# One row of each norm's weights, spread by products with ones, and read-back rows taken one job sooner

## The chip, the core and the metric

The kernel runs on one core of a Trainium2 chip. The metric is the device time of one execution in microseconds, the median over the runs shown. The engines in the text are TensorE (PE, with its weight loads PEld), VectorE (DVE), ScalarE (ACT), GpSimd (POOL) and SyncE (SP, which here issues most of the transfers).

## The reference, cut to what matters

One decoder block on 512 tokens of 1024 values. Two token mixers are merged; their sum with the input goes through a layer norm (LN1). A mixture of 32 experts follows, two experts per token, and a second layer norm (LN2) ends the block.

```python
def layer_norm(x, g, b):
    xf = x.astype(jnp.float32)
    mu = xf.mean(-1, keepdims=True)
    var = jnp.square(xf - mu).mean(-1, keepdims=True)
    return ((xf - mu) * lax.rsqrt(var + LN_EPS) * g.astype(jnp.float32) + b.astype(jnp.float32)).astype(x.dtype)
...
    x = layer_norm(ALPHA * x + merged @ w_out[layer], ln1_g[layer], ln1_b[layer])
    ffn = hier_moe(x, w_group[layer], b_group[layer], w_router[layer], b_router[layer],
                   w_gate[layer], w_up[layer], w_down[layer])
    x = layer_norm(ALPHA * x + ffn, ln2_g[layer], ln2_b[layer])
```

Each of `ln1_g`, `ln1_b`, `ln2_g`, `ln2_b` is one vector of 1024 values. In the kernel a token lies on a partition, so such a vector is wanted on all 128 partitions alike.

## The kernel before

The expert stage takes up the second half of the time. `work` lists 17 jobs, n = 0 to 16: w = 0 to 7, then "ov" (tokens beyond an expert's capacity), then w = 8 to 15. A job w serves experts w and w + 16, with 64 tokens each. It needs six pieces of 1 MB of weights, four up (`w_up`) and two down (`w_dn`). `stage(w)` issues their loads on SP's queue three jobs ahead, each into the next of a ring of pages of 128x2048. Behind the six pieces of w = 15 it issues the two loads of LN2's weights, the last on SP before the output's.

A job's parts on PE have these names in the trace: the up projection `mm<-wexp,xg`; two turns of the hidden activation, `mm<-ident,h`; the transposes of the next job's tokens, `qt<-ident,xg`; the down projection `pv<-wexp,hT`. What a job yields reaches the tokens' rows in one of two ways. Jobs w = 0 to 9 scatter it to `yp` in DRAM (POOL's queue). Jobs w = 10 to 15 combine: the products `qt<-four,ct` put the rows in their places, sixteen of them in eight parts, and DVE adds each part to `acc` (L1293). These parts run during the next job (`late`). "qt" is a ring of four PSUM banks (`qk_bank`), shared by combine products and transposes, so a product waits until an older bank has been read.

The scattered rows come back block by block (b = 0 to 3, 128 tokens each): `back_load` sets a page to zero and gathers twice into it on POOL's queue (L1270, L1271), and `back_add` adds the two halves on DVE (L1278). `BACK_AT` and `BACK_ADD` name the jobs behind which this is written. LN1's weights are applied to `acc` by DVE in jobs 3 to 6 (L1570, L1571). LN2's are `g2`, used from the last job's end on (`centre`, `finish` and `rest`, recorded under L111, as everything else of the last job). In the last job each combine part is added with a running sum (`sums`), LN2's mean follows from these, and block by block the output is written.

The order of instructions on an engine is fixed when the kernel is built: a scheduler places what is written without a fixed place; each engine then works its list in order. A load on SP waits until its page is free and until an older load of its semaphore (eight in turn) has landed.

## Time and profile before

| | |
|---|---|
| median of 3 runs | 690.48 us (690.04 to 690.83) |
| the profiled execution | 689.77 us |
| its span, first to last instruction | 688.0 us |
| PE busy | 648.0 us, 94% |
| DVE busy | 402.8 us, 59% |
| ACT busy | 271.9 us, 40% |
| moved by all queues | 163.23 MB, mean 237 GB/s |

Busy shares are means over the whole span. How PE and the transfers stand to each other in the expert stage is read from windows of that stage, and the end of the kernel from the timelines.

### The profile page before, as it was taken

The page shows a single profiled execution, that of the slowest core. Times are in us where ns is not written, and L with a number is a line of the kernel's source. Part 1 is how long each engine was busy: PE and PEld are TensorE (multiplying, and loading weights), DVE is VectorE, ACT ScalarE, POOL GpSimd, SP SyncE. Part 2 cuts the span into 40 slices and gives each one's busy share as a digit, 9 for nine tenths or more (in the row PEclk, how much of TensorE's full clock was granted, in tenths as well). Part 3 has the DMA queues.
Part 4 walks back from the last instruction along what each step waited for, and adds up shares of the span by engine and source line. Part 5 has one row for each costly group of instructions (what it writes and reads, how often), then busy time and mean ns, then how long its engine had stood idle before and what let it go on. Part 6 is the DMA issues. An engine that isn't in the chain of part 4 may idle for free.

```text
span 688.0 us, 9318 instructions
## 1 busy us (share of the span) xinstructions
PE 648.0 (94%) x3366; PEld 429.1 (62%) x3366; DVE 402.8 (59%) x1016; ACT 271.9 (40%) x600; POOL 105.8 (15%) x111
## 2 busy tenths in 40 slices
PE   8999998999999999999999999999998998998880
PEld 5797886766688887878799993334433342443330
DVE  5785999877455344387725567567224521573783
ACT  5663431859355445464313333122122121322360
POOL 0100000000030000002311002221222120550092
PEclk9999999999999999999999999999999999999995
DMA  8472511011581110243886688999999999999502
GB/s 319 150 258 73 202 62 61 1 62 61 184 306 62 62 62 17 81 149 127 341 329 238 242 315 342 409 418 417 419 420 417 420 420 417 417 416 415 236 31 111
DMA packets 32028, 163.23 MB, mean 237 GB/s; under 512 B 6675, under 2 KB 7963, under 8 KB 16108
## 3 DMA queue, kind: packets, MB, share of 16 engines
q1 hardware_dynamic: 21324, 139.59, 51.2%
q0 software_dynamic: 8560, 19.88, 7.9%
q10 hardware_dynamic: 2096, 3.15, 1.5%
q8 instruction: 27, 0.44, 0.3%
q14 instruction: 21, 0.17, 0.1%
HBM read 156.62 MB, written 17.33 MB: 253 GB/s over the span
## 4 chain that ended last, share of the span: by engine, by line
PE 56%; DMA 26%; DVE 12%; ACT 2%; issue 1%; POOL 1%; SPq 0%; POOLq 0%; ACTq 0%; DVEq 0%
DMA wexp<-in_w_up_dram 10%; DMA wexp<-in_w_dn_dram 10%; PE mm L189 9%; PE mm L191 8%; PE mm L190 8%; PE mm L1118 5%; PE mm L111 3%; DVE pgS L459 3%; PE pv L1118 3%; DVE mx L457 2%; DMA ln<-in_ln_b_dram 2%; PE pv L589 2%; DVE whl L186 2%; DMA wraw<-in_w_in_dram 2%; PE tr L671 1%
## 5 line engine op out<-in xcount | busy, mean ns | idle before, releaser
L1118 PE MATMUL mm<-wexp,xg 128*64 128x512 f32 x448 | 111.9, 602 | 5.5 <-DMA wexp<-in_w_up_dram 5.5
L189 PE MATMUL mm<-xh,whl 128*128 128x512 f32 (+1 forms) x264 | 104.5, 396 | 0.0
L191 PE MATMUL mm<-xh,whl 128*128 128x512 f32 (+1 forms) x264 | 102.6, 389 | 0.0
L190 PE MATMUL mm<-xl,whl 128*128 128x512 f32 (+1 forms) x264 | 102.4, 388 | 0.0
L1118 PEld LDWEIGHTS mm<-wexp,xg 128*64 128x64 f32 x448 | 33.2, 137 | 64.5 <-issue 53.8
L1118 PE MATMUL pv<-wexp,hT 128*64 128x512 f32 x240 | 57.9, 603 | 0.3
L189 PEld LDWEIGHTS mm<-xh,whl 128*128 128x128 f32 x264 | 49.8, 189 | 10.6 <-issue 2.2
L191 PEld LDWEIGHTS mm<-xh,whl 128*128 128x128 f32 x264 | 49.6, 188 | 10.3 <-issue 0.8
L190 PEld LDWEIGHTS mm<-xl,whl 128*128 128x128 f32 x264 | 49.8, 188 | 9.1 <-issue 1.6
L186 DVE TENSOR_TENSOR whl<-wraw,whl 128x1024 fp32r<-128x1024 f32 x34 | 41.5, 1220 | 22.6 <-ACT whl L185 20.8
L1173 ACT ACTIVATE h<-mm 128x256 f32<-128x256 f32 x14 | 5.4, 384 | 100.0 <-PE mm L1118 100.0
L185 ACT ACTIVATE whl<-wraw 128x1024 fp32r<-128x1024 f32 x34 | 35.7, 1053 | 15.3 <-DMA wraw<-in_w_in_dram 11.7
L1175 DVE TENSOR_TENSOR h<-h,mm 128x256 f32<-128x256 f32 x14 | 5.9, 421 | 58.4 <-ACT h L1173 58.4
L1118 PEld LDWEIGHTS pv<-wexp,hT 128*64 128x64 f32 x240 | 18.3, 139 | 32.3 <-issue 29.0
L831 POOL TENSOR_TENSOR tg<-tg 128x512 f32<-128x512 f32 x8 | 12.1, 1517 | 142.0 <-issue 122.5
L1142 ACT ACTIVATE xg<-qt,ln1c 128x128 f32<-128x128 f32 x76 | 28.2, 462 | 12.6 <-PE qt L1118 12.4
L641 DVE CUSTOM_DVE_ANT_0 La<-qk,bias 128x128 f32<-128x128 f32 (+3 forms) x32 | 15.3, 489 | 30.2 <-PE qk L640 27.6
L748 POOL DMA_DIRECT2D yp<-routes x8 | 5.9, 1109 | 153.7 <-DVE routes L735 153.7
L457 DVE MAX8 mx<-pgS 128x8 f32<-128x256 f32 (+2 forms) x48 | 26.6, 554 | 0.7
L1126 POOL MEMSET xg<- 128x1024 f32 x14 | 13.3, 950 | 87.3 <-PE qt L1118 82.6
L1293 DVE TENSOR_TENSOR acc<-acc,qt 128x512 f32<-128x512 f32 x40 | 24.9, 682 | 2.3 <-PE qt L1118 2.2
L111 PE MATMUL mm<-woh,merged 128*128 128x256 f32 x128 | 26.2, 292 | 0.0
(374 smaller groups left out, 1364.0 us busy)
## 6 DMA issues: line engine op xcount, KB each, us to landing
wexp<-in_w_up_dram SPq DMA_DIRECT2D x64, 1024.0 KB
wexp<-in_w_dn_dram SPq DMA_DIRECT2D x31, 1024.0 KB
wraw<-in_w_in_dram SPq DMA_DIRECT2D x16, 1024.0 KB
yp<-routes POOLq DMA_DIRECT2D x8, 512.0 KB, 6.0
braw<-in_w_br_dram SPq DMA_DIRECT2D x4, 1024.0 KB
woraw<-in_w_out_dram SPq DMA_DIRECT2D x4, 1024.0 KB
xraw<-in_xT_dram SPq DMA_DIRECT2D x4, 512.0 KB
skb<-dra POOLq DMA_DIRECT2D x1, 2048.0 KB
```

The source lines that it names most:

```text
L111: i = f(*a, **k)
L185: nc.scalar.activation(hi, raw, AF.Copy)
L186: nc.vector.tensor_sub(lo, raw, hi.bitcast(F32))
L189: nc.tensor.matmul(o, a[0], b[0], start=start, stop=False)
L190: nc.tensor.matmul(o, a[0], b[1], start=False, stop=False)
L191: nc.tensor.matmul(o, a[1], b[0], start=False, stop=stop)
L457: pin(nc.vector.max(out=mx, in_=acc))
L459: pin(nc.vector.match_replace(out=acc, in_to_replace=mx, in_values=acc, imm_value=GONE))
L641: nc.vector.tensor_tensor_reduce(Ls[b], o, ta_bias[h][:, T - n:], 1.0, -3.0e38, ALU.add, ALU.max, m4[:, b:b + 1])
L1118: return lambda *a, **k: (pin if self.n else (lambda i: i))(getattr(nc.tensor, f)(*a, **k))
L1142: nc.scalar.activation(c, src, AF.Identity, scale=g, bias=b_)
L1293: nc.vector.tensor_add(a, a, pc)
```

## The change

LN1's and LN2's weights are no longer loaded to 128 partitions (two loads of 128x1024, 512 KB each, from a source read 128 times). `row_load` brings each vector to one partition (two loads of 1x1024, 4 KB each, into the same page). `row_spread` makes a row of 128 ones on DVE, multiplies it with 512 values of the row at a time on PE (four products, one partition deep, 128x512 out, in banks of the "qt" ring), and ACT copies each result over the page. LN1's spread is written at the end of job 2, LN2's at the end of job 13. Independently, the read-back of blocks 2 and 3 is written one job sooner, and so are all four adds.

```diff
@@ -71,8 +71,9 @@
 
 SCATTER = tuple(range(10))
 K_EARLY = 1
-BACK_AT = {11: (0, 1), 13: (2, 3)}
-BACK_ADD = {13: (0, 1), 14: (2,), 15: (3,)}
+BACK_AT = {11: (0, 1), 12: (2, 3)}
+BACK_ADD = {12: (0,), 13: (1, 2), 14: (3,)}
+LN2_AT = 13
 X1_AT = 3
 LAST_N = (0, 1, 1, 2, 1, 2, 1, 0)
 P_TR = 0
@@ -1384,11 +1385,25 @@
             pg = functools.partial(gather, idx[:, w:w + 1]) if w else None
             load_pieces(6 * w + 6)
             if w == 15:
-                norm2.append(page(F32, "ln2"))
-                nc.sync.dma_start(norm2[0][:, 0:D], bcast(ln2_g, D))
-                nc.sync.dma_start(norm2[0][:, D:2 * D], bcast(ln2_b, D))
+                norm2.append(row_load(ln2_g, ln2_b))
             es = (w, w + 16)
             jobs[w] = (pg, [ups[e] for e in es], [dns[e] for e in es], tok[:, w:w + 1], wsl[:, w:w + 1])
+
+    def row_load(g, b):
+
+        t = page(F32, "ln")
+        for z, v in enumerate((g, b)):
+            nc.sync.dma_start(t[0:1, z * D:(z + 1) * D], v.rearrange("(o d) -> o d", o=1))
+        return t
+
+    def row_spread(t):
+
+        o = temp(F32, "one")[0:1, 0:P]
+        nc.vector.memset(o, 1.0)
+        for c in range(4):
+            ps = qk_bank()
+            nc.tensor.matmul(ps, o, t[0:1, c * T:(c + 1) * T], start=True, stop=True)
+            nc.scalar.activation(t[:, c * T:(c + 1) * T], ps, AF.Copy)
 
     rows_of = {}
 
@@ -1561,9 +1576,11 @@
                 y = down_proj(hT, dn, w_)
                 late = combine(places(tk_), y, then if n + 2 == len(work) else None)
         if n == X1_AT - 2:
-            g1 = page(F32, "ln1")
-            nc.sync.dma_start(g1[:, 0:D], bcast(ln1_g, D))
-            nc.sync.dma_start(g1[:, D:2 * D], bcast(ln1_b, D))
+            g1 = row_load(ln1_g, ln1_b)
+        if n == X1_AT - 1:
+            row_spread(g1)
+        if n == LN2_AT:
+            row_spread(norm2[0])
         if 0 <= n - X1_AT < NB:
 
             a = acc[n - X1_AT]
```

On PE the list of before at jobs 13 and 14 reads as follows (`mm<-wexp,xg 64x512 x16` is one job's up projection, `pv` its down projection; the second one is job 14's).

```order
2169 L1118 MATMUL mm<-wexp,xg 64x512 x16
2170 L1118 MATMUL qt<-four,ct 128x512 x8
2171 L1118 MATMUL mm<-ident,h 128x128 x2
2172 L1118 MATMUL qt<-four,ct 128x512 x8
2173 L1118 MATMUL qt<-ident,xg 128x128 x8
```

Of the changed kernel it reads, at the same job 14:

```order
2171 L1119 MATMUL mm<-wexp,xg 64x512 x16
2172 L1119 MATMUL mm<-ident,h 128x128 x2
2173 L1405 MATMUL qt<-ln,one 128x512 x4
2174 L1119 MATMUL qt<-four,ct 128x512 x16
2175 L1119 MATMUL qt<-ident,xg 128x128 x8
```

LN2's four products (`qt<-ln,one`) stand behind the turns of h, and all sixteen combine products, eight of which stood ahead of the turns, now stand behind them.

On DVE, from job 13's hidden activation to the last job's first partial sum, before (`acc<-acc,back` are the adds of read-back rows, two for each block, `acc<-acc,qt` the combine's):

```order
753 L1175 TENSOR_TENSOR h<-h,mm 128x256
754 L1293 TENSOR_TENSOR acc<-acc,qt 128x512 x8
755 L1282 TENSOR_SCALAR ct<-iot,tok 128x512
756 L1278 TENSOR_TENSOR acc<-acc,back 128x1024 x2
...
769 L1218 SCALAR_TENSOR_TENSOR four<-pv,wsl,four 128x512 x2
770 L1278 TENSOR_TENSOR acc<-acc,back 128x1024 x2
771 L1293 TENSOR_TENSOR acc<-acc,qt 128x512 x2
772 L1278 TENSOR_TENSOR acc<-acc,back 128x1024 x2
773 L111 TENSOR_TENSOR g_5465<-iot,routes 128x128 x4
774 L111 ISA acc,sums<-acc,qt 128x512
```

And of the changed kernel, from the same place:

```order
754 L1176 TENSOR_TENSOR h<-h,mm 128x256
755 L1294 TENSOR_TENSOR acc<-acc,qt 128x512 x2
756 L1279 TENSOR_TENSOR acc<-acc,back 128x1024
757 L1294 TENSOR_TENSOR acc<-acc,qt 128x512
758 L1279 TENSOR_TENSOR acc<-acc,back 128x1024
759 L1294 TENSOR_TENSOR acc<-acc,qt 128x512 x5
...
767 L1294 TENSOR_TENSOR acc<-acc,qt 128x512 x8
768 L1279 TENSOR_TENSOR acc<-acc,back 128x1024 x2
769 L1219 SCALAR_TENSOR_TENSOR four<-pv,wsl,four 128x512 x2
770 L1176 TENSOR_TENSOR h<-h,mm 128x256
```

The adds of block 0 moved in among job 13's eight combine adds, and the last two pairs moved out of the last job, ahead of job 15's hidden activation. SP's and POOL's lists keep their order.

## Rows read from the trace of the kernel before

**Rows 1.** The page's first line: span and instructions.
```profile
span 688.0 us, 9318 instructions
```

**Rows 2.** Windows: per stretch busy us (count) by engine, granted clock, DMA share, GB/s.
```profile
540.00:580.00 40.00, 36.38 (x170) 14.69 (x171) 10.93 (x30) 9.24 (x22) 7.93 (x8) 0.96 1.02 418
580.00:620.00 40.00, 40.00 (x184) 19.07 (x180) 23.44 (x36) 10.65 (x26) 20.31 (x20) 1.00 1.02 417
620.00:640.00 20.00, 17.79 (x82) 8.30 (x82) 7.62 (x14) 5.44 (x14) 0.00 (x0) 1.00 1.01 414
640.00:642.00 2.00, 2.00 (x11) 0.71 (x12) 0.00 (x0) 2.00 (x7) 0.00 (x0) 1.00 0.86 356
...
650.00:652.00 2.00, 0.79 (x4) 0.00 (x0) 1.98 (x6) 0.00 (x0) 0.00 (x0) 1.00 0.15 61
652.00:654.00 2.00, 1.29 (x4) 0.59 (x6) 1.96 (x7) 1.31 (x3) 0.59 (x1) 0.77 0.03 10
654.00:656.00 2.00, 2.00 (x5) 0.50 (x2) 1.54 (x7) 2.00 (x4) 2.00 (x3) 0.50 0.00 0
656.00:658.00 2.00, 2.00 (x8) 0.73 (x6) 1.26 (x4) 2.00 (x5) 2.00 (x2) 0.87 0.02 4
```

**Rows 3.** The chain that ended last, 560 to 690: start, us, what.
```profile
635.63 15.52 DMA ln<-in_ln_b_dram
```

**Rows 4.** PE's timeline from 590: start, us, instructions, [idle before <- what ended it].
```profile
617.61 2.12 PE L1118 MATMUL qt<-four,ct 128*128 128x512 f32 x8
619.56 1.18 PE L1118 MATMUL qt<-ident,xg 128*128 128x128 f32 x8
...
630.68 3.65 PE L1118 MATMUL mm<-wexp,xg 128*64 128x512 f32 x14 [1.89 <-DMA wexp<-in_w_up_dram]
...
638.75 1.26 PE L1118 MATMUL qt<-ident,xg 128*128 128x128 f32 x8 [0.32 <-DVE acc L1293]
...
643.42 1.89 PE L111 MATMUL mm<-wexp,xg 128*64 128x512 f32 x8
...
652.71 0.92 PE L111 MATMUL qt<-four,ct 128*128 128x512 f32 x2 [1.92 <-DVE sums L111]
```

**Rows 5.** DVE's timeline, from 450 (first row) and from 590.
```profile
455.90 2.35 DVE L1570 TENSOR_TENSOR acc<-acc,ln 128x1024 f32<-128x1024 f32 x2
...
599.86 4.87 DVE L1293 TENSOR_TENSOR acc<-acc,qt 128x512 f32<-128x512 f32 x8
...
608.44 1.23 DVE L1278 TENSOR_TENSOR acc<-acc,back 128x1024 f32<-128x1024 f32 x1 [1.78 <-DMA back<-yp,bidx]
...
645.05 2.47 DVE L1278 TENSOR_TENSOR acc<-acc,back 128x1024 f32<-128x1024 f32 x2
...
648.76 2.48 DVE L1278 TENSOR_TENSOR acc<-acc,back 128x1024 f32<-128x1024 f32 x2
...
661.64 0.47 DVE L111 SCALAR_TENSOR_TENSOR h<-h,wsl,mm 128x256 f32<-128x256 f32 x1
```

**Rows 6.** SP's timeline from 440, and one of its waits (us, times, longest).
```profile
608.67 3.60 SPq L789 DMA_DIRECT2D wexp<-in_w_dn_dram  x2
...
627.69 3.33 SPq L789 DMA_DIRECT2D wexp<-in_w_dn_dram  x2
633.21 0.33 SPq L1388 DMA_DIRECT2D ln<-in_ln_g_dram  x1
635.63 0.33 SPq L1389 DMA_DIRECT2D ln<-in_ln_b_dram  x1
```
```profile
SPq L1388 <- DMA wexp<-in_w_dn_dram: 2.0, 1, 2.0
```

**Rows 7.** Groups by line and form: busy us, mean ns of one, idle before.
```profile
L406 PE MATMUL qk<-ohp,relx 33*8 33x512 f32 x2 | 1.0, 589 | 0.0
...
L1217 ACT ACTIVATE four<-pv,wsl 128x512 fp32r<-128x512 f32 x10 | 7.0, 703 | 11.7 <-PE pv L1118 11.7
```

## The prediction

> **What bounds the kernel now.** I start at the profiled execution's own time, 689.77 us: a span of 688.0 [rows 1] and 1.77 us around it. The sum below is made against the span; the median of the runs shown, 690.48, lies 0.7 above that execution.

> Next come the windows. From 540 to 640 us the DMA share is 1.01 to 1.02 and 414 to 418 GB/s move, while PE is busy 36.38 of 40, 40.00 of 40 and 17.79 of 20 us [rows 2]. So in the middle of the expert stage both are near full, and the transfers are slightly the tighter: the chain that ended last runs through expert weights up to 635.63, and then through the last LN2 load for 15.52 us, to 651.15 [rows 3]. After 640 the stream of weights dries up, unevenly: the share is 0.86 at 640 to 642, 0.15 at 650 to 652, 0.03 at 652 to 654 [rows 2]. Some engines have nothing left more than ten microseconds before others.

> PE's timeline then gives the fixed stretches of the end. The second half of job 14's combine ends at 619.56, where the transposes for job 15 begin; the last job's up projection begins at 643.42, and in between PE waits 1.89 us for a weight piece and 0.32 for an add; in the last job it waits 1.92 for DVE [rows 4]. On DVE, the hidden activation of the last job runs at 661.64 [rows 5]; from there to the end of the span are 26.36 us of LN2.

> **What the change does, part by part.**

> *Bytes.* Each norm's load falls from two of 512 KB to two of 4 KB. 1.05 MB at 418 GB/s [rows 2] are 2.5 us, once for LN1 (everything SP issues afterwards lands up to 2.5 us sooner) and once for LN2, at the stream's very end. LN2's rows are still the last loads on SP, behind all six pieces of w=15. Today they are issued at 633.21 and 635.63, the first after a wait of 2.0 us for an earlier down piece to land, and the issue of w=15's down pieces is at 627.69 [rows 6]. With 2.5 us taken off, the first row is issued no sooner than 630.7.

> *The LN2 products.* This is the part that decides. Before, nothing on PE needed LN2's weights. Now four products read them, and the order of PE places these in job 14, right behind the two turns of h and ahead of all sixteen combine products. In the trace of before that place is at 617.61 [rows 4], 615.1 with the 2.5 us. PE works in order, so it stands there until the row has landed, and behind it stand the combine, the transposes, the down projection, all of job 15 and the last job. DVE's adds and ACT's evacuations wait for PE in turn. SP is not held: w=15's pieces reuse pages that are free before this place.

> When does the row land? Lower bound: its issue at 630.7 and a little, say 633. Upper bound: when everything ahead of it in the queue is in. The chain has the last landing at 651.15 [rows 3]; less 2.5 for LN1 and 2.5 for LN2's own bytes this is 646.1. By the windows the last bytes arrive shortly after 652 [rows 2], up to 653, which would make it 648. I take 646.1, so PE stands still for about 646.1 - 615.1 = 31 us.

> *What follows the wait.* Four fp32 products of one row of ones by 512 columns. No such row is in the trace; the nearest has 33 rows and 512 columns, two records that cover 1.0 us together, 0.59 each [rows 7]. A product thus costs 0.6 to 1.0; I take 0.8, so 3.2 us. The four ACT copies of 128x512 cost about 0.70 each [rows 7] and run beside the next products and the combine. Then sixteen combine products, twice the 8 that take from 617.61 to 619.56, 1.95 us [rows 4], give 3.9; DVE's eight adds behind them need 4.87 in all [rows 5], so I add 0.2. [...] From the first product to the transposes: 3.2 + 4.1 + 1.7 = 9.0.

> From the transposes to the last job: 643.42 - 619.56 - 1.89 - 0.32 = 21.65, since all weights are in by then.

> *The back adds.* Four adds of 128x1024, 2.47 and 2.48 us, leave DVE in the last job [rows 5] and move ahead. The first partial sums of LN2 are then no longer late, so PE's 1.92 goes, and with it that dip of the clock, 1.7: the hidden activation comes 661.64 - 643.42 - 3.6 = 14.6 us after the start of the last up projection. The two adds for block 0 now stand in job 13 behind the second and the third of the combine's eight adds. There they wait for their gather: today the second one can start only at 608.44, while the eight adds ran from 599.86 [rows 5]. The five left would end at about 608.44 + 1.23 + 5 x 0.61 = 612.7 in place of 604.7, and PE, whose banks these adds free, is late by up to 8 us. That delay ends inside the 31 us wait and costs nothing; without that cover it would cost most of its size.

> *The LN1 products.* 3.2 us of PE early in job 3, at about 458 us. The data is there (DVE used it from 455.90 without a wait [rows 5]). PE's idle 3.6 us of the stretch 540 to 580 [rows 2] takes them up: nothing.

> *Sum.* 646.1 + 9.0 + 21.65 + 14.6 + 26.36 = 717.7 us of span, and 1.77 around it: 719.5.

> **Rivals.**

> *A, the forecast:* the row comes after the whole queue. 719.5, and with the bounds of landing (646.1 to 648) and of the products (0.6 to 1.0 each) 718.7 to 722.2. For it: the order on SP; the chain.

> *B: the row lands before the queue as a whole is dry.* For it: engines run dry at times spread over more than ten microseconds [rows 2], and 4 KB in one partition need not wait for the slowest one if they travel on one engine alone. In the windows half of the share is gone about halfway between 640 and 652, at 646 us; less 5.0 that is 641. This gives 714.4; from 633 to 646.1 the time runs from 706.4 to 719.5. Against it: the row may be cut over all engines, or sit on the slowest. No load of one partition is in the trace. [...]

> *C: no wait at the LN2 products,* because the row would be in SBUF when PE comes by. Then the change gains: 688.0 - 1.89 - 0.32 - 3.6 + 3.2 = 685.4 of span, 687.2 us, faster by 0.5%, as long as the adds in job 13 don't lose it again (up to 8 us: 695). It decides at a landing before about 615 to 623. SP's rows speak against it: the issue alone is later than that [rows 6], and only a queue that ran 8 us or more ahead of before could change it.

> *D: longer than A,* over 722. After such a pause PE could stay at the low clock for more than the 6 us that the windows show, or DVE's adds could come out as the tighter in the combine and in job 15. Each further 2 us at 0.50 cost 1.

> **How the numbers follow.** A 0.50, B 0.42, C 0.03, D 0.05. The time is A's, 719.5. The range takes in B down to 707 (rows that land within a microsecond of their issue are left out) and A up to 722.5. About 0.2%, 1.4 us, is what can be told from no change here. A, B and D are all slower by 2% or more. Of C's 0.03 two thirds are faster, the rest same or slower: faster 0.02, same 0.01, slower 0.97.

> **What would show it.** In the profile after: an idle time of PE of 15 to 32 us, beginning at 615 to 623, released by the DMA of LN2's row, in front of the products of ones; LN2's issues on SP at 630 to 634; no add of read-back rows on DVE in the last job, and no wait of PE for the partial sums there; DMA share at 1.0 up to about 636 and nothing of weights after 648; a low granted clock for some microseconds where PE resumes; a wait of DVE for a gather in job 13; 1.05 MB less for each norm. I am wrong if PE passes the products without a wait (then by all of it), if the wait ends before 633, or if the last stretch from transposes to the end is not 62 to 63 us long.

## The result, and the profile after

The changed kernel takes 721.45 us, the median of 4 runs (721.31 to 722.14), against 690.26 for the kernel before: a ratio of 1.0456, 95% interval 1.0438 to 1.0474. Forecast were 719.5 us, 707.0 to 722.5. The profiled execution took 722.14 us with a span of 720.0.

SP's timeline answers to [rows 6]: start, us, instruction.

```profile
631.22 0.28 SPq L1396 DMA_DIRECT2D ln<-in_ln_g_dram  x1
634.19 0.23 SPq L1396 DMA_DIRECT2D ln<-in_ln_b_dram  x1
```

The two LN2 rows are still the last loads, issued 2.0 and 1.4 us sooner than the loads of before. PE's timeline answers to [rows 4], from the wait in job 13 to the last job:

```profile
611.01 0.81 PE L1119 MATMUL qt<-four,ct 128*128 128x512 f32 x2 [2.80 <-DVE acc L1294]
...
617.69 7.03 PE L1119 MATMUL mm<-wexp,xg 128*64 128x512 f32 x32
625.69 0.44 PE L1119 MATMUL mm<-ident,h 128*128 128x128 f32 x2 [0.97 <-DVE h L1176]
646.29 7.19 PE L1405 MATMUL qt<-ln,one 1*128 1x512 f32 x8 [20.16 <-DMA ln<-in_ln_g_dram]
653.41 6.66 PE L1119 MATMUL qt<-four,ct 128*128 128x512 f32 x16
659.91 1.04 PE L1119 MATMUL qt<-ident,xg 128*128 128x128 f32 x8
...
680.02 1.89 PE L112 MATMUL mm<-wexp,xg 128*64 128x512 f32 x8
```

PE comes to the LN2 products (eight records, four products) at 626.13 and stands for 20.16 us until the row of `g` has landed, at 646.29. Then the products take 7.19 us and the combine's sixteen 6.66, where eight of them took 2.12 before [rows 4]. From the transposes (659.91) on all weights are there. The chain that ended last, answering to [rows 3], names the same transfer:

```profile
631.22 15.03 DMA ln<-in_ln_g_dram
...
646.29 7.19 PE qt L1405 x8
```

The windows answer to [rows 2] (stretch, its length, busy us and count of PE, PEld, DVE, ACT and POOL, granted clock, DMA share, GB/s):

```profile
640.00:642.00 2.00, 0.00 (x0) 0.00 (x0) 0.00 (x0) 0.00 (x0) 0.00 (x0) 0.50 0.64 266
...
646.00:648.00 2.00, 1.71 (x2) 0.83 (x3) 0.00 (x0) 0.00 (x0) 0.00 (x0) 0.50 0.15 61
648.00:650.00 2.00, 2.00 (x4) 0.80 (x3) 0.00 (x0) 0.60 (x1) 0.00 (x0) 0.50 0.03 12
650.00:658.00 8.00, 8.00 (x16) 4.49 (x15) 2.75 (x4) 1.79 (x3) 0.00 (x0) 0.50 0.00 0
658.00:660.00 2.00, 2.00 (x8) 1.54 (x7) 1.73 (x3) 0.00 (x0) 0.00 (x0) 0.67 0.00 0
```

The granted clock is at 0.50 not only while PE stands (640 to 642) but for 13 us after it resumes (0.67 from 658 to 660). And the transfers are not over when PE resumes: the mean share of the 16 DMA engines is still 0.15 from 646 to 648, and 0.03 from 648 to 650. On DVE, the second add of block 0 waits for its gather among job 13's combine adds, and the last job has no add of read-back rows (answers to [rows 5]):

```profile
609.14 1.22 DVE L1279 TENSOR_TENSOR acc<-acc,back 128x1024 f32<-128x1024 f32 x1 [1.71 <-DMA back<-yp,bidx]
...
693.68 0.47 DVE L112 SCALAR_TENSOR_TENSOR h<-h,wsl,mm 128x256 f32<-128x256 f32 x1
```

### The profile page after: what moved, and what is told of

It reads as the page before. It is cut to its first block, busy times and chain, and to the rows that moved or that the text cites. A ratio compares the mean times of both kernels' runs of the same rounds, so it can differ in the third digit from the quotient of the medians.

```text
span 720.0 us, 9358 instructions
## 1 busy us (share of the span) xinstructions
PE 663.7 (92%) x3382; PEld 438.2 (61%) x3382; DVE 403.1 (56%) x1018; ACT 276.7 (38%) x608; POOL 104.7 (15%) x111
## 5 line engine op out<-in xcount | busy, mean ns | idle before, releaser
L1119 PE MATMUL pv<-wexp,hT 128*64 128x512 f32 x240 | 59.9, 618 | 0.3
L186 ACT ACTIVATE whl<-wraw 128x1024 fp32r<-128x1024 f32 x34 | 35.7, 1054 | 15.6 <-DMA wraw<-in_w_in_dram 11.9
L1405 PE MATMUL qt<-ln,one 1*128 1x512 f32 x16 | 10.9, 838 | 20.2 <-DMA ln<-in_ln_g_dram 20.2
L1119 PE MATMUL qt<-four,ct 128*128 128x512 f32 x72 | 23.5, 462 | 4.6 <-DVE acc L1294 3.8
```

What stands on the lines that cost most here:

```text
L186: nc.scalar.activation(hi, raw, AF.Copy)
L1119: return lambda *a, **k: (pin if self.n else (lambda i: i))(getattr(nc.tensor, f)(*a, **k))
L1405: nc.tensor.matmul(ps, o, t[0:1, c * T:(c + 1) * T], start=True, stop=True)
```

## The experiments

Medians of all runs; the ratio is to the kernel before, run on the same chip beside each. Line numbers of the changed kernel and of the experiments are a few higher than those of before.

**The landing of the row, moved.** The LN2 rows go ahead of w = 15's pieces on SP, in the second kernel ahead of w = 14's (`w == 14`):

```diff
-            load_pieces(6 * w + 6)
             if w == 15:
                 norm2.append(row_load(ln2_g, ln2_b))
+            load_pieces(6 * w + 6)
```

> The two LN2 rows are issued on SP ahead of the six pieces of w=15 instead of behind them; nothing else differs from the changed kernel, PE's order included. Theory (PE stands in front of the LN2 products until the row lands, and the row lands behind the backlog of its queue): issue at about 612.5, landing 15 to 24 us later, 628 to 637, so PE waits 2 to 11 us from 626.1 in place of 20.2 and the time falls by 9 to 18 us and some of the low clock's price, to 700 to 712. Rival (the place of the products and what follows them costs it, not the landing): no change, 721.

Measured: 705.51 us (1.0225, 1.0203 to 1.0247). SP's issue, and PE's wait:

```profile
612.88 0.28 SPq L1396 DMA_DIRECT2D ln<-in_ln_g_dram  x1
```
```profile
630.33 7.19 PE L1405 MATMUL qt<-ln,one 1*128 1x512 f32 x8 [5.41 <-DMA ln<-in_ln_g_dram]
```

With PE's list unchanged, the row lands 16.0 us sooner and the time falls by 15.9: as long as PE waits there, the time follows the landing.

> The LN2 rows are issued ahead of the six pieces of w=14, one job earlier still; the products then stand behind job 13's down projection, ahead of job 14's up projection. Theory: the row lands by 618, PE does not wait for it, and what is left of the change shows: PE 7 us late in job 13 (the adds of block 0 wait for their gather), 3.7 us of products twice, against a shorter last job. From the changed kernel's rows: 617.7 + 3.7 + 11.9 + 20.1 + 13.7 + 26.3 = 693.4 of span, 695 us, range 690 to 697. Rival (the rest of the change gains as soon as the wait is gone): 687 or less.

Measured: 698.79 us (1.0123, 1.0106 to 1.014), runs from 695.92 to 700.5, 1.8 over the range expected; the profiled one is the fastest of them.

```profile
614.76 3.70 PE L1405 MATMUL qt<-ln,one 1*128 1x512 f32 x8
618.39 8.78 PE L1119 MATMUL mm<-wexp,xg 128*64 128x512 f32 x32
```

No wait is left at the products, and they take 3.70 us. But the up projection behind them takes 8.78 us in place of 7.03 (the granted clock reads 0.65 and 0.50 in the two stretches of 2 us from 618), PE still waits 1.00 and 2.23 us for adds in job 13, and the time is 8 us over that of before. So 22.7 of the 31 us go with the wait and the low clock behind it, and the rest of the change does not gain once the wait is gone.

**One part at a time.** LN2's weights loaded to 128 partitions again, without a spread (LN1's row and the read-back stay as changed):

```diff
-                norm2.append(row_load(ln2_g, ln2_b))
+                norm2.append(page(F32, "ln2"))
+                nc.sync.dma_start(norm2[0][:, 0:D], bcast(ln2_g, D))
+                nc.sync.dma_start(norm2[0][:, D:2 * D], bcast(ln2_b, D))
...
-        if n == LN2_AT:
-            row_spread(norm2[0])
```

> LN2's weights are loaded to 128 partitions as before and not spread; LN1's row and the earlier read-back stay. Theory (all 31 us are the wait at the LN2 products): 687 to 692; the adds in job 13 cost up to 7 us on PE, the last job gives back 5. From the changed kernel's rows without products and wait: 617.7 + 11.9 + 20.1 + 13.7 + 26.3 = 689.7 of span, 691.5 us. Rival (read-back or LN1 carry part of the loss by themselves): over 694.

Measured: 692.76 us (1.0041, 1.0023 to 1.0058), runs from 689.19 to 696.0, and 0.8 over the range expected. 28.7 of the 31 us hang on LN2's row and its spread. The other way round, LN2's row alone (`BACK_AT`, `BACK_ADD` and LN1 as before):

> LN2's row and its spread alone; LN1 as before and read-back as before. Theory (the wait ends when the LN2 row lands, whatever PE did before): LN1's 2.5 us of transfers are back, so the row lands at 648 to 649 and the time is 721.5 + 2.5 = 724. Rival (the parts add up, with PE's lateness in job 13 in the sum): 714 to 718, since PE is not late in job 13.

Measured: 723.14 us (1.047, 1.0453 to 1.0488).

```profile
620.15 0.44 PE L1119 MATMUL mm<-ident,h 128*128 128x128 f32 x2 [0.93 <-DVE h L1176]
647.70 7.19 PE L1405 MATMUL qt<-ln,one 1*128 1x512 f32 x8 [27.11 <-DMA ln<-in_ln_g_dram]
```

PE comes 5.5 us sooner than in the changed kernel and stands 7 us longer; the end follows the landing, not PE's arrival. Read-back alone (both norms as before):

```diff
-BACK_AT = {11: (0, 1), 13: (2, 3)}
-BACK_ADD = {13: (0, 1), 14: (2,), 15: (3,)}
+BACK_AT = {11: (0, 1), 12: (2, 3)}
+BACK_ADD = {12: (0,), 13: (1, 2), 14: (3,)}
```

> Read-back and adds one job sooner, alone; both norms' weights as before. Theory (block 0's adds stand among job 13's combine adds and wait there for a gather, PE waits for the banks; the last job is shorter in return): PE 5 to 8 us late in job 13 against 3.6 us of the last job and 2 to 4 us of waits for weights that the lateness hides: 689 to 694, and more spread between runs than before, since the gather's landing decides. Rival (the earlier adds only gain): 685 to 688.

Measured: 690.83 us (1.001, 0.9997 to 1.0022). In job 13 PE waits for DVE's adds, which wait for the gather:

```profile
603.08 0.73 PE L1119 MATMUL qt<-four,ct 128*128 128x512 f32 x2 [1.00 <-DVE acc L1294]
606.43 0.74 PE L1119 MATMUL qt<-four,ct 128*128 128x512 f32 x2 [2.63 <-DVE acc L1294]
```

What job 13 loses, the last job gives back: no difference. LN1's row alone:

> LN1's row and spread alone; LN2 and read-back as before. Theory (3.7 us of products on PE are taken up by its waits for weights, which the 2.5 us of transfers saved make shorter by as much): 688.5 to 691, no change that can be told. Rival (PE is the bound behind job 3, so the products cost their full 3.7): 693 to 694. Rival (the transfers bound it: 2.5 are gained): 688.

Measured: 690.11 us (0.9989, 0.9978 to 1.0001). No difference either.

**One engine or all.** Each row's load is cut into 16 runs of 64 values, stored with gaps; the products read the runs, and ACT writes to a page of its own:

```diff
         t = page(F32, "ln")
+        r = t[0:1].rearrange("p (a z c) -> p a z c", a=16, z=2)
         for z, v in enumerate((g, b)):
-            nc.sync.dma_start(t[0:1, z * D:(z + 1) * D], v.rearrange("(o d) -> o d", o=1))
+            nc.sync.dma_start(r[:, :, z], v.rearrange("(o a c) -> o a c", o=1, a=16))
...
```

> The changed kernel with each row's load cut into 16 runs of 256 bytes, stored with gaps so that they stay 16 runs, and the products' results put into a page of their own; places on SP and PE as in the changed kernel. Theory (4 KB as one run ride on one engine and land when that engine is through, at 646.3, while others still carry weights until 649 to 650): with 16 engines the row lands with the last of them, 3 us later: 724 to 725. Rival (the row already comes behind the whole queue): 721 to 722.

Measured: 724.89 us (1.0498, 1.0483 to 1.0513), 3.4 over the changed kernel. In its profiled execution (the fastest of its runs, 723.47) the row is issued at 630.66, 0.6 sooner than in the changed kernel, and PE resumes 2.3 later, just when the DMA share has reached 0.00:

```profile
648.55 7.19 PE L1408 MATMUL qt<-ln,one 1*128 1x512 f32 x8 [25.88 <-DMA ln<-in_ln_g_dram]
```
```profile
646.00:648.00 2.00, 0.00 (x0) 0.00 (x0) 0.00 (x0) 0.00 (x0) 0.00 (x0) 0.50 0.08 33
648.00:650.00 2.00, 1.45 (x2) 0.83 (x3) 0.00 (x0) 0.00 (x0) 0.00 (x0) 0.50 0.00 0
```

The packets of SP's queue (packets, MB, share; the changed kernel first) say on how many engines a row lies:

```profile
q1 hardware_dynamic: 20756, 137.51, 47.9%
```
```profile
q1 hardware_dynamic: 20876, 137.51, 48.1%
```

The four rows have 120 packets more, 30 each, when they are cut in 16. In the trace of the changed kernel the uncut row of `g` is 2 packets, one of 4 KB (645.62 to 645.78) and one of 4 bytes behind it, and its semaphore is updated once, at 646.25; the last weight piece of 1 MB updates its own 16 times, from 635.49 to 649.40. An estimate from this is 32 packets for a cut row, 16 of data and 16 of 4 bytes, 30 more than 2; the packets of the run itself are shown only as a sum. Read as one update for each engine, a row in one run rides on one engine and lands before the queue is dry, and one in 16 runs lands when it is dry (share 0.00 from 648 to 650). LN2's row alone agrees: there the uncut row lands at 647.70, and the share is still 0.17 from 648 to 650.

**Read-back sooner, adds where they were.** The kernel before, with `BACK_AT = {11: (0, 1), 12: (2, 3)}` and nothing else:

> The kernel before with nothing changed but the read-back of blocks 2 and 3, written at job 12 in place of 13; the adds stay at jobs 13 to 15. On DVE the adds of blocks 0 and 1 stand as before, those of block 2 move into job 14, those of block 3 ahead of the last job's hidden activation. Theory (the last job loses its wait of 1.92 us for the sums and the dip of the clock behind it, 1.7 us, and no add waits in job 13): 690.5 - 3.6 = 687, range 686 to 688.5. Rival (the end of the last job is set by the transfers' end, or an add waits elsewhere): 690 to 691.

Measured: 686.16 us (0.9931, 0.9918 to 0.9944), faster than both kernels. On DVE block 3's adds now stand before the last job's partial sums, where DVE had time:

```profile
635.98 4.87 DVE L1294 TENSOR_TENSOR acc<-acc,qt 128x512 f32<-128x512 f32 x8
...
641.15 2.48 DVE L1279 TENSOR_TENSOR acc<-acc,back 128x1024 f32<-128x1024 f32 x2
```

PE no longer waits for the sums in the last job, and its clock stays at 1.00 there. With LN1's row on top:

> The read-back sooner with the adds kept (686.2) and LN1's row and spread. Theory (LN1's products and the transfers that they save cancel, as in the run of LN1 alone): 685.5 to 688, no change against 686.2 that can be told. Rival (with the last job shorter the transfers bound it, so 2.5 are gained): 684.

Measured: 685.09 us (0.9922, 0.9908 to 0.9935), the fastest kernel of the study; 0.4 under the range expected. Its interval and that of the run without LN1's row overlap, so LN1's row is worth one microsecond or nothing.

**The whole change, mended.** LN2's rows ahead of w = 14's pieces, and adds where they were:

> Both rows and both spreads, the LN2 row issued ahead of w=14's pieces (the products stand behind job 13's down projection), and the read-back sooner with the adds kept: the whole change without its two waits. Theory (3.7 us of products for LN2 fall into a stretch in which PE is the bound by then, and its 2.5 us of transfers are no longer waited for): 688 to 691, better than the changed kernel by 31 to 33, and not better than the read-back alone (686.2). Rival (the transfers saved are worth their full 5 us): 682 to 684.

Measured: 692.36 us (1.0024, 1.001 to 1.0038), a miss of 1.4 us over the range. The profiled execution (the slowest of its runs, 695.7) shows that the row was late here too:

```profile
612.12 7.16 PE L1405 MATMUL qt<-ln,one 1*128 1x512 f32 x8 [3.17 <-DMA ln<-in_ln_g_dram]
619.22 10.03 PE L1119 MATMUL mm<-wexp,xg 128*64 128x512 f32 x32
```

3.17 us of wait, 7.16 of products and an up projection of 10.03 in place of 7.04. The row costs more on PE than its 2.5 us of transfers bring: the kernel just above differs from this one only in LN2's row and its spread, and is 7.3 us faster (685.09). And the kernel with the row ahead of w = 14's pieces and the adds one job sooner differs from it in the adds alone, and is 6.4 us slower (698.79).

**The clock.** In the changed kernel PE does 22 products more ahead of job 14's up projection, whose result nobody uses:

```diff
...
+        if busy:
+            ps = qk_bank()
+            for k in range(busy):
+                nc.tensor.matmul(ps, ident, iot, start=True, stop=True)
+            nc.vector.tensor_copy(mv4[:, 0, 0:1], ps[:, 0:1])
...
-            row_spread(norm2[0])
+            row_spread(norm2[0], 22)
```

> The changed kernel with 22 more products (the identity by a table of 128x512, their result is not used), which PE does ahead of job 14's up projection, so that it is busy, not idle, in most of the time in which the LN2 row is on its way. They should take about 20 us, and PE should come to the LN2 products at 645 to 648, about when the row lands (646). Theory (the low granted clock behind the long wait makes the products 7.2 in place of 3.7 us and the combine 6.7 in place of 4.1): both fall back, and the time falls by 5 to 6 us although PE does 20 us more, to 715 to 718. Rival (the products and the combine are slow there for another reason, the banks of the ring or the copies on ACT): 721 or more.

Measured: 718.9 us (1.0403, 1.0385 to 1.0421), 2.6 less than the changed kernel for 19 us of work more, and less gain than expected. The theory is half right. PE comes to the LN2 products with the clock at 1.00 and waits 2.78 us there, but the clock falls in the middle of them and stays low through the combine:

```profile
615.25 19.15 PE L1404 MATMUL qt<-iot,ident 128*128 128x512 f32 x44
...
645.58 5.85 PE L1410 MATMUL qt<-ln,one 1*128 1x512 f32 x8 [2.78 <-DMA ln<-in_ln_g_dram]
651.36 6.64 PE L1119 MATMUL qt<-four,ct 128*128 128x512 f32 x16
```
```profile
644.00:646.00 2.00, 0.42 (x1) 0.29 (x2) 0.00 (x0) 0.00 (x0) 0.00 (x0) 1.00 0.23 94
646.00:648.00 2.00, 2.00 (x5) 0.88 (x4) 0.00 (x0) 0.60 (x1) 0.00 (x0) 0.74 0.08 33
648.00:656.00 8.00, 8.00 (x16) 4.49 (x15) 2.75 (x4) 1.79 (x3) 0.00 (x0) 0.50 0.00 0
656.00:658.00 2.00, 2.00 (x8) 1.53 (x8) 1.81 (x3) 0.00 (x0) 0.00 (x0) 0.70 0.03 8
```

So it is not the pause alone. The changed kernel shows the same behind LN1's products, with no pause at all (PE's timeline and windows there; PE is busy all the time):

```profile
460.10 3.69 PE L1405 MATMUL qt<-ln,one 1*128 1x512 f32 x8
```
```profile
460.00:464.00 4.00, 4.00 (x11) 1.60 (x12) 1.25 (x2) 1.96 (x4) 0.00 (x0) 1.00 1.02 423
464.00:466.00 2.00, 2.00 (x8) 0.53 (x6) 2.00 (x2) 0.43 (x1) 0.00 (x0) 0.69 1.01 416
466.00:468.00 2.00, 2.00 (x7) 0.55 (x4) 1.38 (x2) 0.00 (x0) 0.00 (x0) 0.50 1.03 430
```

This dip does not come every time. Nine profiles have LN1's products of one row: in six of them the clock falls in the products or behind them (to 0.50 also with the row ahead of w = 14, from 462 to 464, with LN1's row alone, from 464 to 466, and with LN1's row and the adds kept, from 466 to 468), in three (LN2 as before, 16 runs, the whole change mended) it stays at 1.00. In the last of these, with the same eight records at 459.49:

```profile
464.00:466.00 2.00, 2.00 (x11) 0.70 (x8) 2.00 (x3) 0.00 (x0) 0.00 (x0) 1.00 1.01 416
```

The last run makes each spread product 128 rows deep, 127 of them zeros:

```diff
         t = page(F32, "ln")
+        nc.gpsimd.memset(t, 0.0)
...
-        o = temp(F32, "one")[0:1, 0:P]
+        o = temp(F32, "one")[:, 0:P]
...
-            nc.tensor.matmul(ps, o, t[0:1, c * T:(c + 1) * T], start=True, stop=True)
+            nc.tensor.matmul(ps, o, t[:, c * T:(c + 1) * T], start=True, stop=True)
```

> The changed kernel, but each spread product is 128 rows deep in place of one: the page is set to zero ahead of the row's load, and the ones fill 128x128, so the sum is the same row. PE's order and the number of products are the changed kernel's. Theory (products of one row do not keep PE's granted clock up: it fell in the middle of busy work behind LN1's products, and it came back only some microseconds behind the LN2 products): the dip behind LN1's products at 465 is gone, and behind the wait the clock is back before the products end, so that products and combine take about 5 and 4.5 us in place of 7.2 and 6.7: 716 to 718.5. Rival (the clock comes back after a fixed time of PE's new start, whatever it multiplies): the dip at 465 may go, but the time stays at 721 to 722.

Measured: 724.72 us (1.0497, 1.0483 to 1.0512): the time missed the range, and the reason held in part. There is no dip behind LN1's products, which shows little by itself, since three kernels with products of one row have none either. Behind the wait the clock is back about when the products end:

```profile
464.00:466.00 2.00, 2.00 (x12) 0.71 (x9) 2.00 (x2) 0.32 (x1) 0.00 (x0) 1.00 1.05 434
466.00:468.00 2.00, 2.00 (x11) 0.95 (x9) 1.61 (x3) 0.45 (x2) 0.00 (x0) 1.00 0.97 408
...
656.00:658.00 2.00, 2.00 (x5) 0.86 (x3) 0.00 (x0) 0.79 (x2) 0.00 (x0) 0.59 0.00 0
658.00:660.00 2.00, 2.00 (x9) 1.49 (x8) 1.14 (x2) 0.60 (x1) 0.00 (x0) 1.00 0.00 0
```
```profile
651.80 6.57 PE L1406 MATMUL qt<-ln,one 128*128 128x512 f32 x8 [27.45 <-DMA ln<-in_ln_g_dram]
657.81 4.32 PE L1119 MATMUL qt<-four,ct 128*128 128x512 f32 x16
662.00 1.25 PE L1119 MATMUL qt<-ident,xg 128*128 128x128 f32 x8
```

The clock is back 5.8 us after PE resumed. With products of one row it took 10.7 to 13.0 us, in all five kernels in which PE resumed with them after a wait at the lower clock. From the first product to the transposes 10.2 us pass in place of 13.6. But SP waits for the page to be set to zero at LN1's row, 11.3 us, its pieces and with them LN2's row come later, and the row lands 5.5 us later, at 651.80:

```profile
SPq L1397 <- POOL ln L1395: 11.3, 1, 11.3
```

## Why the prediction was right, step by step

**The LN2 products** (31 us of wait, ending at 646.1): right in place and cause, and in its end by luck (next point). The wait ends at 646.29. It is 20.2 us long, not 31, because PE comes 11 us later than assumed: 2.5 us sooner than before was assumed, and it comes 8.5 later (626.13 against 617.61). At job 14's up projection it is 10.0 us behind before (617.69 against 607.66), of which 3.75 are there at job 13's and 6.3 come in job 13; the eight combine products that stood ahead of this place and now stand behind it give part of that back. That this lateness costs nothing is what the run of LN2's row alone shows: LN2's row alone, with PE earlier, is no faster.

**When the row lands**: the number was right by luck, its reason was not. The forecast A took 646.1 as the end of the whole queue. The queue was dry about 3 us later (share 0.03 from 648 to 650), and the row landed about 3 us ahead of that. So it came as in rival B, on one engine, but late in B's range: of the last weight piece's 16 updates 13 came before the row's at 646.25, and three after it (647.47 to 649.40). The end of the queue, put 3 us too early, and the row, put behind the whole queue, cancelled. The run with 16 runs per row separates the two: it waits for the dry queue and is 3.4 us slower. That an uncut row sits on one engine was rival B's condition, and nothing had shown it when it was forecast; the runs bear it out, with the landing at 646.29 against 648.55 us for the row cut in 16, with 30 packets fewer, and with one update where a weight piece has 16. Which engine it is, no run here shows. B's 714.4 failed in its guess of 641 for the landing.

**What follows the wait** (9.0 us): mis-sized, 13.6. The products were put at 3.2 us and are 3.7 at the full clock (LN1's, 3.69); the combine at 4.1 is right at the full clock (4.2 in the last run). The low clock was put at 1.7, from the dip behind a wait of 1.92 in the last job: what is missing from 1.00 at 0.77, 0.50 and 0.87, times 2 us [rows 2, 4]. It cost 13.62 - 3.7 - 4.2 = 5.7, since it lasted 13 us after PE resumed.

**From the transposes to the last job** (21.65): 20.11. I took off the wait for weights, but not what it did to the up projection: in two pieces around the wait it took 4.63 and 3.65 us before, in one piece 7.04, which is 1.24 of the 1.54.

**The back adds** (14.6 from the last up projection to the hidden activation): 13.66. The 1.92 and the dip are gone as forecast; the first LN2 instruction on DVE, which stood ahead of it with 1.94 us, takes 1.01. The adds in job 13 waited as forecast (PE for 1.00 and 2.80 us, and it loses 6.3 us in that job, where up to 8 was forecast), and under the cover of the wait they cost nothing. Without that cover they cost all that the last job gains: alone, the read-back change measures 1.001, and with the adds left in place 0.9931.

**The LN1 products** (nothing): right in sum, alone 0.9989. Their cover is not as large as assumed: PE's busy time from 540 to 580 rises from 36.38 to 39.55 us, and PE is still 3.75 us behind at job 13's up projection (595.75 against 592.00).

**The sum**: 717.7 of span was forecast, 720.0 came: 646.29 + 13.62 + 20.11 + 13.66 + 26.32. The errors, +0.2, +4.6, -1.5, -0.9 and 0.0, cancel in part. Two signs named in the prediction failed: the wait began at 626.1 (615 to 623 was named), and the stretch from the transposes to the end is 60.1 us long. The prediction named 62 to 63 for it and called another length a sign of being wrong; the terms of 21.65 and 14.6 are the ones that were too long. Rival C (no wait) is answered by the kernels with the row ahead of w = 14: they too end over the kernel before. One thing stays open: read-back and LN1 together cost 2.1 us more than before (692.76 against 690.67), though neither does alone. The runs narrow it down: with the adds left in place LN1's row costs nothing (0.9922 against 0.9931), with the adds one job sooner it goes with 1.0041 against 1.001, two intervals that barely part. So it would be the earlier adds, not the earlier reads, that do not go well with LN1's row. That the two share one cover, PE's few waits for weights, would explain it, but was only argued.

## What to carry to other kernels

Here a transfer's size did not set when it landed; what was queued ahead of it did: 4 KB took 15.0 us behind pieces of 1 MB. Before a load is moved under an engine that works in order, look up in that engine's list where its first reader stands, and in the trace when the load is issued: 28.7 of the 31 us hung on LN2's row, and 22.7 came back once it was issued ahead of w = 14's pieces. Where an edit has two halves, one that reads sooner and one that adds sooner, try them apart: reading sooner alone was the gain, 4.6 us, and adding sooner gave it back.
